# Weight-stationary tiles of a hybrid GLA and pooling backbone: all hi products of both units first, then all lo products

## Chip, core and metric

One Trainium2 chip, one core. The metric is the device time of one execution in microseconds. The kernel before takes 1768.76 us, the median of 3 runs (1768.55 to 1773.19).

## What is computed

One layer (DEPTH = 1) of a backbone on 256 latent tokens and 256 context tokens, width 2048, all in float32. Cut to what matters:

```python
sh_m, sc_m, gt_m, sh_f, sc_f, gt_f = split(silu(c) @ w_ada + b_ada, 6)   # the same for c_ctx
h_lat, h_ctx = x * (1 + sc_m) + sh_m, ctx * (1 + csc_m) + csh_m
q, k, v, g, a_lr, p, bg = split(h @ w_in)           # latent and context tokens
o_l = two-way chunked gated linear attention over latent tokens, started from the context's state
y_gla  = (rms_norm(o_l) * gain * silu(g)) @ w_gla_out
y_pool = (concat((box_mean(p_i) - p_i) @ w_pool_group[i]) * pool_scale) @ w_pool_out
mix = (sigmoid(bg_1) * y_gla + sigmoid(bg_2) * y_pool) @ w_out
x = layer_norm(2 ** 0.25 * x + gt_m * mix)
gate, up = split((x * (1 + sc_f) + sh_f) @ w_ffn_in)
x = layer_norm(2 ** 0.25 * x + gt_f * ((silu(gate) * up) @ w_ffn_out))
```

## The kernel before

**Precision by two parts.** A float32 factor is split into hi (rounded to TensorE's fp32r by ScalarE, L97) and lo, the rest (VectorE, L98). A product is hi*hi + hi*lo + lo*hi. Activations are kept as [hi | lo] side by side, 2 x 256 columns.

**Two kinds of matmul blocks.** In `nat_block` (L143 on; v, g, p, w_out, FFN out) activations are stationary and weights stream. In `ws_tile` (L116 to L134) weights are stationary: one tile gives 128 output columns, and its weights come in units of 128 x 1024, eight blocks of 128 rows of the contraction. For each unit the hi block streams the whole activation (a wide matmul, 512 columns, hi*hi and hi*lo, L127), the lo block only the activation's hi half (a narrow one, 256 columns, L131); `fold` (L136 to L141) adds the two halves of the PSUM bank afterwards, ScalarE first, then VectorE. `ws_tile` serves the stages k (8 tiles of two units, each for two activations, latent and context), q (8 tiles), gates, GLA output and pool output (16 column steps with two gate tiles, one GLA tile and one pool tile of a single unit each), and FFN in (44 steps with a gate tile and an up tile). All but the pool output's tiles have two units.

**Buffers.** `weights` (L101 on) issues the load of a unit into raw (L93, on SyncE's queue) and splits it into hi and lo. Each of raw, hi and lo has three buffers in the pool wp, shared by both kinds of blocks: a raw buffer comes free when lo is computed, a hi or lo buffer when TensorE has used it.

**What sets the order.** Instructions are written in program order and a scheduler orders each engine's queue by it and by what is ready; the splits are raised by 200 places (`tc.high_priority(PW)`), and some work is tied behind others (`tc.issue_after`). Beside the matmuls VectorE works off the rest of the adaLN projection in multiply-sums (L270, weights "ra" on SyncE's queue; in the FFN L930, "fa"), a few per tile. `bcast_cols` (L780 on) turns a modulation column into rows: VectorE writes diagonal tiles dg (L789), eight in all, and TensorE multiplies each with ones (L791); this happens at the start of w_out and again near the end of FFN in. Ahead of FFN in, `finish_mix` (L877 on) transposes the normed x, modulates it (L886, L889) and splits it into h, whose first half holds contraction blocks 0 to 7, whose second half 8 to 15.

Of the kernel before, what the change touches and what calls it, by code (L numbers as in the profile page):

```python
# [15 lines left out]
P = 128  # L16
D = 2048
KT = D // P
T = 256
# [39 lines left out]
def trunk(ctx, tc, small, masks, xT, ctxT, x_nat, lnrows, wdec, pmat, c_row,  # L59
# [5 lines left out]
    PE = nc.tensor  # L65
# [17 lines left out]
    def nm(s):  # L83
        cnt[0] += 1
        return f"{s}{cnt[0]}"

    def bank(kind="d"):
        pool, n = psum[-1]
        return pool.tile([P, 512], F32, tag=kind, bufs=n if kind == "d" else 8 - n, name=nm("ps"))

    def raw_unit(src, eng=None):
        r = wp.tile([P, U], F32, tag="raw", name=nm("raw"))
        (eng or nc.sync).dma_start(r, src)  # L93
        return r

    def split(full, hi, lo):
        S.activation(hi, full, AF.Copy)  # L97
        last_split[:] = [V.tensor_tensor(lo, full, hi.bitcast(F32), op=ALU.subtract)]  # L98
        return last_split[0]

    def weights(src):  # L101
        r = raw_unit(src)
        hi = wp.tile([P, U], F32R, tag="hi", name=nm("hi"))
        lo = wp.tile([P, U], F32R, tag="lo", name=nm("lo"))
        with tc.high_priority(PW):
            split(r, hi, lo)
        return hi, lo
# [8 lines left out]
    def ws_tile(srcs, acts, nk, kind="d"):  # L116

        outs = [bank(kind) for _ in acts]  # L120
        n = 0
        for src in srcs:
            hi, lo = weights(src)
            m = min(8, nk - n)
            for j in range(m):
                for o, act in zip(outs, acts):
                    PE.matmul(o, hi[:, j * P:(j + 1) * P], act(n + j), start=(n + j == 0), stop=(n + j == nk - 1),  # L127
                              skip_group_check=True)
            for j in range(m):
                for o, act in zip(outs, acts):  # L130
                    PE.matmul(o[:, :T], lo[:, j * P:(j + 1) * P], act(n + j)[:, :T], start=False, stop=(n + j == nk - 1),  # L131
                              skip_group_check=True)
            n += m
        return outs  # L134

    def fold(dst, o, scale=None):  # L136
# [6 lines left out]
    def nat_block(srcs, acts, k0=0, after=None, last=None, pre=None, cols=None):  # L143


        cols = cols or [(0, 512)] * len(acts)
        outs = [bank()[:, :c1 - c0] for c0, c1 in cols]
        n = k0
        end = k0 + 2 * len(srcs) - 1 if last is None else last
        for src in srcs:  # L150
            hi, lo = weights(src)
            if pre:
                pre()
            parts = [(j, o, act(n + j), j * 512 + c0, j * 512 + c1)
                     for j in range(2) for o, act, (c0, c1) in zip(outs, acts, cols)]
            for j, o, (ah, al), a, b in parts:
                PE.matmul(o, ah, hi[:, a:b], start=(n + j == k0), stop=False)  # L157
                PE.matmul(o, al, hi[:, a:b], start=False, stop=False)  # L158
            for j, o, (ah, al), a, b in parts:
                last_mm[:] = [PE.matmul(o, ah, lo[:, a:b], start=False, stop=(n + j == end))]  # L160
            n += 2
            if after:
                after()
        return outs
# [62 lines left out]
    with ExitStack() as c1:  # L227
# [27 lines left out]
        def ada(n, last=96):  # L255
            for _ in range(n):
                u = ada_next[0]
                if u >= last or not ada_pool:
                    return
                half, i = divmod(u, 48)  # L260
                if half not in silb:
                    silb[half] = p1.tile([P, U], F32, tag="silb", name=nm("silb"))
                    silu_row(silb[half], half, last_load[0])
                    return
                ada_next[0] += 1
                pool, tag, bufs = ada_pool[-1]
                r = pool.tile([P, U], F32, tag=tag, bufs=bufs, name=nm("ra"))
                nc.sync.dma_start(r, w_adaT[64 * half + i])
                with tc.issue_after(last_split[0].ins):
                    V.scalar_tensor_tensor(r, r, 1.0, silb[half], op0=ALU.mult, op1=ALU.mult,  # L270
                                           accum_out=mods[:, half, i:i + 1])
# [63 lines left out]
        def step(n=1):  # L335
            for _ in range(n):
                while pending:
                    try:
                        next(pending[0])
                        break  # L340
                    except StopIteration:
                        pending.pop(0)
# [24 lines left out]
        for n in GROUPS.values():  # L367
            for b in range(4):
                outs = nat_block([w_v[8 * b + a // 2 + i] for i in range(n // 2)], lat_s + ctx_s, k0=a,
                                 after=lambda: (step(STEPS[a]), ada(ADA[0].get(a, 0))))  # L370
# [46 lines left out]
        def kT_half(b):  # L417
            for lst, n in ((kT, "kT"), (kTc, "kTc")):
                if b == 0:
                    both[n] = sl(n)  # L420
                lst.append(both[n][:, b])
            for i in range(4):
                n = 2 * (4 * b + i)
                outs = ws_tile([w_k[n], w_k[n + 1]], [lat_m, ctx_m], KT)
                fold(kT[b][:, i, :], outs[0])
                fold(kTc[b][:, i, :], outs[1])
                if b == 0 and i == 0:
                    decay_rows()
                else:
                    ada(ADA[1])  # L430

        def qT_half(b):
            if b == 0:
                both["qT"] = sl("qT")
            qT.append(both["qT"][:, b])
            for i in range(4):
                n = 2 * (4 * b + i)
                o, = ws_tile([w_q[n], w_q[n + 1]], [lat_m], KT)
                fold(qT[b][:, i, :], o, HK ** -0.5)
# [262 lines left out]
        for b in range(2):  # L702
# [3 lines left out]
            for c in range(4):  # L706
                o = bank("g")
                for t in range(2):
                    PE.matmul(o[:, :T], p_blocks[b][:, t, c * P:(c + 1) * P], pm[:, t, c // 2, :],  # L709
                              start=(t == 0), stop=(t == 1))  # L710
# [26 lines left out]
        for ct in range(KT):  # L737
            o1, = ws_tile([w_bg[2 * ct + j] for j in range(2)], [lat_m], KT)
            yt = py.tile([P, 2 * T], F32, tag="tmp", bufs=2, name=nm("yt"))
            ys = py.tile([P, 2 * T], F32, tag="tms", bufs=2, name=nm("ys"))  # L740
            sg = yt[:, :T]
            fold(sg, o1)
            S.activation(sg, sg, AF.Sigmoid)
            if ct == 0:
                pool_out(0)
            o2, = ws_tile([w_bg[32 + 2 * ct + j] for j in range(2)], [lat_m], KT)
            sp = yt[:, T:]
            if ct == 0:
                pool_out(1)
            fold(sp, o2)  # L750
            last_sig[:] = [S.activation(sp, sp, AF.Sigmoid)]
            o3, = ws_tile([w_go[2 * ct + j] for j in range(2)], [moving(lambda kt: og[kt // 4][:, kt % 4])], KT)
            fold(ys[:, :T], o3)
            V.tensor_tensor(sg, ys[:, :T], sg, op=ALU.mult)
            o4, = ws_tile([w_po[ct]], [moving(lambda kt: yp[kt // 4][:, kt % 4])], 8)
            fold(ys[:, T:], o4)
            V.tensor_tensor(sp, ys[:, T:], sp, op=ALU.mult)
            V.tensor_tensor(sg, sg, sp, op=ALU.add)
            m = mT[ct // 8][:, ct % 8]
            split(sg, m[:, 0, :], m[:, 1, :])  # L760
            ada(ADA[2] if ct < 15 else 128)
# [86 lines left out]
    for b in range(3):  # L848
        outs = nat_block([w_o[8 * b + i] for i in range(8)], m_s)
# [91 lines left out]
    for b in range(3):  # L941
        outs = nat_block([w_fo[22 * b + i] for i in range(22)], hid_s)
# [6 lines left out]
    def finish_ffn(t):  # L949
        mean, rs = mv_rs[t]  # L950
        for b in range(4):
# [6 lines left out]
    outs = nat_block([w_fo[66 + i] for i in range(18)], [hid_s[t] for t, _, _ in PARTS], last=NF - 1,  # L958
                     cols=[c for _, *c in PARTS])
# [129 lines left out]
```

## Time and profile before

| | before |
|---|---|
| median of 3 runs | 1768.76 us (1768.55 to 1773.19) |
| the profiled execution's own time | 1772.31 us |
| its span, first to last instruction | 1770.5 us |
| mean granted TensorE clock | 0.992 |
| busy: TensorE, VectorE, ScalarE | 98%, 66%, 45% |
| moved from HBM | 389.58 MB, 221 GB/s over the span |

Stages in the profiled execution, from the span's start: adaLN and v to about 234 us, k to about 331, q with attention and g to about 590, gates and outputs to about 919, w_out and the first norm to about 1018, FFN in to about 1512, FFN out and the last norm to the end.

PE stands for TensorE's matmuls and PEld for its weight loads, DVE for VectorE, ACT for ScalarE, SP for SyncE. The end of a matmul in the records is modelled and overlaps the next one's start, so distances are taken from start to start. A bracket behind a row gives the idle time ahead of it and what ended it.

### The profile page before, as it was taken

What the parts mean: (1) busy time and instruction counts of PE and PEld (TensorE: products, weight loads), DVE (VectorE), ACT (ScalarE), POOL (GpSimd) and SP (SyncE); (2) the same over time, 40 slices, a digit from 0 to 9 for tenths busy, and PEclk for the clock granted to TensorE, in tenths of its full rate; (3) what the DMA queues carried; (4) which work ended last, traced back from release to release, by engine and by line L of the source; (5) the groups of instructions that cost most, each with busy time, mean ns of one, the idle gap of its engine ahead of it and who ended that gap; (6) DMA issues with size and microseconds to landing.
All of it is one profiled execution on the core that took longest, in us unless ns stands there. A gap on an engine that the chain in (4) does not pass through costs nothing.

```text
span 1770.5 us, 24390 instructions
## 1 busy us (share of the span) xinstructions
PE 1730.5 (98%) x9407; PEld 1451.1 (82%) x9407; DVE 1170.1 (66%) x1661; ACT 800.3 (45%) x1173; POOL 11.5 (1%) x28
## 2 busy tenths in 40 slices
PE   9999999999999999999999899999999999999996
PEld 5667888887777888888887788888888888888886
DVE  3667866667875677777776756666666666554455
ACT  2223132565874544444444554445444444443332
POOL 0000010000000000000000000000000000000000
PEclk9999999999999999999999999999999999999998
DMA  9797757443334478777785445577777766555553
GB/s 391 292 354 259 258 210 278 159 157 126 110 120 178 157 267 284 267 258 275 278 306 192 155 166 188 186 264 246 248 236 248 233 236 221 192 192 194 196 190 120
DMA packets 109059, 393.26 MB, mean 222 GB/s; under 512 B 12144, under 2 KB 12272, under 8 KB 108432
## 3 DMA queue, kind: packets, MB, share of 16 engines
q1 hardware_dynamic: 107424, 384.25, 62.4%
q0 software_dynamic: 1520, 7.47, 1.2%
q8 instruction: 73, 1.20, 0.3%
q14 instruction: 42, 0.34, 0.1%
HBM read 389.58 MB, written 2.10 MB: 221 GB/s over the span
## 4 chain that ended last, share of the span: by engine, by line
PE 87%; DVE 6%; ACT 3%; DMA 2%; issue 2%; SPq 0%; ACTq 0%; DVEq 0%
PE ps L127 34%; PE ps L131 18%; PE ps L157 10%; PE ps L160 10%; PE ps L158 10%; PE ps L293 2%; DVE lo L98 1%; DMA raw<-in_w_o 1%; ACT hi L97 1%; DMA raw<-in_w_fi 1%; PE ps L581 1%; DMA rw<-in_w_sh_sc 1%; PE ps L571 0%; PE ps L409 0%; PE ps L709 0%
## 5 line engine op out<-in xcount | busy, mean ns | idle before, releaser
L98 DVE TENSOR_TENSOR lo<-raw,hi 128x1024 fp32r<-128x1024 f32 x510 | 623.7, 1224 | 432.9 <-ACT hi L97 420.8
L97 ACT ACTIVATE hi<-raw 128x1024 fp32r<-128x1024 f32 x510 | 539.2, 1058 | 674.0 <-PE ps L127 275.1
L127 PE MATMUL ps<-h,hi 128*128 128x512 f32 x1408 | 353.4, 392 | 0.8 <-DVE h L98 0.8
L127 PEld LDWEIGHTS ps<-h,hi 128*128 128x128 f32 x1408 | 253.3, 189 | 46.5 <-DVE h L98 1.2
L127 PE MATMUL ps<-hl,hi 128*128 128x512 f32 x768 | 210.3, 392 | 0.0
L131 PEld LDWEIGHTS ps<-h,lo 128*128 128x128 f32 x1408 | 192.5, 190 | 13.9
L131 PE MATMUL ps<-h,lo 128*128 128x256 f32 x1408 | 196.8, 282 | 0.0
L127 PEld LDWEIGHTS ps<-hl,hi 128*128 128x128 f32 x768 | 139.4, 189 | 25.3
L157 PE MATMUL ps<-hi,hid 128*128 128x512 f32 (+1 forms) x372 | 134.9, 369 | 0.0
L158 PE MATMUL ps<-hi,hid 128*128 128x512 f32 (+1 forms) x372 | 134.0, 369 | 0.0
L157 PE MATMUL ps<-hi,hl 128*128 128x512 f32 x320 | 128.7, 403 | 2.7 <-ACT hi L97 2.7
L158 PE MATMUL ps<-hi,hl 128*128 128x512 f32 x320 | 126.6, 396 | 0.0
L270 DVE SCALAR_TENSOR_TENSOR ra<-ra,silb 128x1024 f32<-128x1024 f32 x96 | 114.4, 1221 | 13.0 <-DMA ra<-in_w_adaT 12.9
L131 PE MATMUL ps<-hl,lo 128*128 128x256 f32 x768 | 120.5, 282 | 0.0
L131 PEld LDWEIGHTS ps<-hl,lo 128*128 128x128 f32 x768 | 111.7, 190 | 6.9
L160 PE MATMUL ps<-lo,hl 128*128 128x512 f32 x320 | 93.0, 391 | 0.1
L160 PE MATMUL ps<-lo,hid 128*128 128x512 f32 x372 | 90.6, 369 | 0.0
L157 PEld LDWEIGHTS ps<-hi,hid 128*128 128x128 f32 x372 | 69.8, 188 | 12.1 <-DVE xt L812 0.2
L158 PEld LDWEIGHTS ps<-hi,hid 128*128 128x128 f32 x372 | 70.0, 188 | 11.9
L157 PEld LDWEIGHTS ps<-hi,hl 128*128 128x128 f32 x320 | 60.3, 189 | 22.5 <-issue 5.2
L348 DVE TENSOR_TENSOR v<-ps,v 128x512 f32<-128x512 f32 x80 | 50.7, 685 | 39.8 <-PE ps L160 39.7
L160 PEld LDWEIGHTS ps<-lo,hid 128*128 128x128 f32 x372 | 66.2, 188 | 11.9
(259 smaller groups left out, 2045.0 us busy)
## 6 DMA issues: line engine op xcount, KB each, us to landing
raw<-in_w_fi SPq DMA_DIRECT2D x176, 512.0 KB, 4.2
ra<-in_w_adaT SPq DMA_DIRECT2D x96, 512.0 KB, 4.9
raw<-in_w_fo SPq DMA_DIRECT2D x88, 512.0 KB, 4.3
rw<-in_w_sh_sc SPq DMA_DIRECT2D x64, 512.0 KB, 7.4
raw<-in_w_bg SPq DMA_DIRECT2D x64, 512.0 KB, 4.8
raw<-in_w_v SPq DMA_DIRECT2D x32, 512.0 KB, 5.7
raw<-in_w_g SPq DMA_DIRECT2D x32, 512.0 KB, 3.5
raw<-in_w_go SPq DMA_DIRECT2D x32, 512.0 KB, 4.2
```

The lines of the kernel that those rows point to most:

```text
L97: S.activation(hi, full, AF.Copy)
L98: last_split[:] = [V.tensor_tensor(lo, full, hi.bitcast(F32), op=ALU.subtract)]
L127: PE.matmul(o, hi[:, j * P:(j + 1) * P], act(n + j), start=(n + j == 0), stop=(n + j == nk - 1), skip_group_check=True)
L131: PE.matmul(o[:, :T], lo[:, j * P:(j + 1) * P], act(n + j)[:, :T], start=False, stop=(n + j == nk - 1), skip_group_check=True)
L157: PE.matmul(o, ah, hi[:, a:b], start=(n + j == k0), stop=False)
L158: PE.matmul(o, al, hi[:, a:b], start=False, stop=False)
L160: last_mm[:] = [PE.matmul(o, ah, lo[:, a:b], start=False, stop=(n + j == end))]
L270: V.scalar_tensor_tensor(r, r, 1.0, silb[half], op0=ALU.mult, op1=ALU.mult, accum_out=mods[:, half, i:i + 1])
L293: mm = PE.matmul(pr[32 * g:32 * g + 32, :256], sil[:, kt, :], r[:, 256 * g:256 * g + 256], start=(u == 0), stop=(u == KT // per - 1), skip ...
L348: V.tensor_tensor(dst, src, dst, op=ALU.add)
L581: PE.matmul(scc[:, t * T:(t + 1) * T], kst[:, c, t * P:(t + 1) * P], q4[:, c].rearrange("p t i -> p (t i)"), start=(d == 0 and c == 0 and ...
```

## The change

`ws_tile` fetches the weights of both units first (`ws`), then runs the products in two passes: s = 0 over all hi blocks of both units, s = 1 over all lo blocks. A one-unit tile keeps its order. Nothing else is edited, and the number and shapes of all instructions stay.

```diff
         outs = [bank(kind) for _ in acts]
-        n = 0
-        for src in srcs:
-            hi, lo = weights(src)
-            m = min(8, nk - n)
-            for j in range(m):
+        ws = [weights(src) for src in srcs]
+        for s in range(2):
+            for n in range(nk):
+                w = ws[n // 8][s][:, n % 8 * P:n % 8 * P + P]
                 for o, act in zip(outs, acts):
-                    PE.matmul(o, hi[:, j * P:(j + 1) * P], act(n + j), start=(n + j == 0), stop=(n + j == nk - 1),
-                              skip_group_check=True)
-            for j in range(m):
-                for o, act in zip(outs, acts):
-                    PE.matmul(o[:, :T], lo[:, j * P:(j + 1) * P], act(n + j)[:, :T], start=False, stop=(n + j == nk - 1),
-                              skip_group_check=True)
-            n += m
+                    if s == 0:
+                        PE.matmul(o, w, act(n), start=(n == 0), stop=(n == nk - 1), skip_group_check=True)
+                    else:
+                        PE.matmul(o[:, :T], w, act(n)[:, :T], start=False, stop=(n == nk - 1), skip_group_check=True)
         return outs
```

Lines behind it move up by four; a narrow matmul is L131 before and L129 after. TensorE's queue at the start of FFN in, before (h_8309 and h_8310 are the first and the second half of the activations; hi and lo with their number are one unit's two parts; a row ends with the number of equal matmuls):

```order
L127 MATMUL ps_8627<-h_8309,hi_8630 128x512 x4
L127 MATMUL ps_8676<-h_8309,hi_8679 128x512
L127 MATMUL ps_8627<-h_8309,hi_8630 128x512 x4
L131 MATMUL ps_8627<-h_8309,lo_8631 128x256 x8
L127 MATMUL ps_8676<-h_8309,hi_8679 128x512 x7
L131 MATMUL ps_8676<-h_8309,lo_8680 128x256 x7
L127 MATMUL ps_8627<-h_8310,hi_8652 128x512 x8
L131 MATMUL ps_8627<-h_8310,lo_8653 128x256 x8
L131 MATMUL ps_8676<-h_8309,lo_8680 128x256
L127 MATMUL ps_8676<-h_8310,hi_8701 128x512 x8
L131 MATMUL ps_8676<-h_8310,lo_8702 128x256 x8
```

The same place after:

```order
L127 MATMUL ps_8627<-h_8309,hi_8630 128x512 x4
L127 MATMUL ps_8676<-h_8309,hi_8679 128x512
L127 MATMUL ps_8627<-h_8309,hi_8630 128x512 x4
L127 MATMUL ps_8676<-h_8309,hi_8679 128x512 x7
L127 MATMUL ps_8627<-h_8310,hi_8636 128x512 x4
L127 MATMUL ps_8676<-h_8310,hi_8685 128x512 x3
L127 MATMUL ps_8627<-h_8310,hi_8636 128x512 x4
L129 MATMUL ps_8627<-h_8309,lo_8631 128x256 x8
L129 MATMUL ps_8627<-h_8310,lo_8637 128x256 x8
L127 MATMUL ps_8676<-h_8310,hi_8685 128x512 x5
L129 MATMUL ps_8676<-h_8309,lo_8680 128x256 x8
L129 MATMUL ps_8676<-h_8310,lo_8686 128x256 x8
```

The 15 narrow matmuls that stood ahead of the first use of h_8310 now stand behind it; in the later tiles 16 wide ones stand together, then 16 narrow ones. ScalarE's queue at that place (ht to h is a split of activations), before:

```order
L889 ACTIVATE ht_8619<-ps_8614,fcol 128x128 x4
L97 ACTIVATE hi_8701<-raw_8699 128x1024
L97 ACTIVATE h_8310<-ht_8607 128x4x128
L97 ACTIVATE h_8310<-ht_8619 128x4x128
L97 ACTIVATE hi_8729<-raw_8727 128x1024
L97 ACTIVATE hi_8751<-raw_8749 128x1024
```

And after:

```order
L885 ACTIVATE ht_8619<-ps_8614,fcol 128x128 x4
L97 ACTIVATE hi_8685<-raw_8683 128x1024
L97 ACTIVATE h_8310<-ht_8607 128x4x128
L97 ACTIVATE hi_8729<-raw_8727 128x1024
L97 ACTIVATE h_8310<-ht_8619 128x4x128
L97 ACTIVATE hi_8735<-raw_8733 128x1024
```

A weight split has moved between the two last splits of the activations. VectorE's queue at the second broadcast, near the end of FFN in (dg_12878 and dg_12881 are the first two diagonal tiles, ps_12821 the tile that TensorE ends just ahead of them), before:

```order
L789 TENSOR_TENSOR dg_12878<-sm,fs_12874 128x512
L98 TENSOR_TENSOR lo_12913<-raw_12910,hi_12912 128x1024
L140 TENSOR_TENSOR sg_12817<-ps_12772,sg_12817 128x256
L98 TENSOR_TENSOR lo_12935<-raw_12932,hi_12934 128x1024
L98 TENSOR_TENSOR lo_12962<-raw_12959,hi_12961 128x1024
L140 TENSOR_TENSOR sg_12817<-ps_12821,sg_12817 128x256
L789 TENSOR_TENSOR dg_12881<-sm,fs_12874 128x512
```

And after:

```order
L98 TENSOR_TENSOR lo_12913<-raw_12910,hi_12912 128x1024
L136 TENSOR_TENSOR sg_12817<-ps_12772,sg_12817 128x256
L785 TENSOR_TENSOR dg_12878<-sm,fs_12874 128x512
L98 TENSOR_TENSOR lo_12919<-raw_12916,hi_12918 128x1024
L98 TENSOR_TENSOR lo_12962<-raw_12959,hi_12961 128x1024
L136 TENSOR_TENSOR sg_12817<-ps_12821,sg_12817 128x256
L785 TENSOR_TENSOR dg_12881<-sm,fs_12874 128x512
```

The first dg has moved behind a lo tile and a fold, the second keeps its place on VectorE. On TensorE the second dg's matmul stood behind 8 wide and 4 narrow matmuls of the next tile; it now stands behind 11 wide ones:

```order
L787 MATMUL ps_12877<-dg_12878,onesq 128x512
L127 MATMUL ps_12909<-h_8309,hi_12912 128x512 x8
L127 MATMUL ps_12909<-h_8310,hi_12918 128x512 x3
L787 MATMUL ps_12877<-dg_12881,onesq 128x512
L127 MATMUL ps_12909<-h_8310,hi_12918 128x512 x4
```

The seventh dg's matmul there follows eight wide matmuls that need a new unit; on VectorE two lo tiles stand ahead of that dg.

## The prediction

> **What bounds the kernel now.** I read the page first (busy shares and the chain that ended last), then the busy time by stretches, then the timeline of short stretches and the chain in order of time. From the page:
>
> ```profile
> PE 1730.5 (98%) x9407; PEld 1451.1 (82%) x9407; DVE 1170.1 (66%) x1661; ACT 800.3 (45%) x1173; POOL 11.5 (1%) x28
> PE 87%; DVE 6%; ACT 3%; DMA 2%; issue 2%; SPq 0%; ACTq 0%; DVEq 0%
> ```
>
> TensorE is busy almost throughout and carries 87% of the chain. The busy time by stretches (columns: stretch and length, then busy time and count of PE, PEld, DVE, ACT and POOL, granted clock, DMA share, GB/s) shows the two long weight-stationary stages, the gate and output projections and the first FFN matrix:
>
> ```profile
> 590.00:919.00 329.00, 329.00 (x1887) 289.53 (x1886) 243.64 (x344) 162.32 (x239) 1.05 (x2) 1.00 0.78 265
> 1018.00:1512.00 494.00, 492.02 (x2811) 432.31 (x2812) 328.99 (x446) 244.28 (x366) 1.58 (x3) 1.00 0.66 224
> ```
>
> There PE hardly rests and the clock is full, so two things can move the time: how densely the matmuls follow each other, and a wait of PE that comes or goes. With one activation a unit is 8 wide matmuls (hi, 512 columns) and 8 narrow ones (lo, 256 columns), and a tile is two units. The timeline of the FFN stage (start, length modelled to the end of the last matmul, engine) shows four units, two tiles:
>
> ```profile
> 1099.81 2.00 PE L127 MATMUL ps<-h,hi 128*128 128x512 f32 x8
> 1101.65 1.12 PE L131 MATMUL ps<-h,lo 128*128 128x256 f32 x8
> ...
> 1105.39 2.00 PE L127 MATMUL ps<-h,hi 128*128 128x512 f32 x8
> ...
> 1110.98 2.00 PE L127 MATMUL ps<-h,hi 128*128 128x512 f32 x8
> ```
>
> From start to start a wide run takes 1.84 us and a unit 2.79; the two tiles take 11.17, so 5.59 each.
>
> **Term 1: fewer steps between narrow and wide.** The number and shapes of the matmuls stay. A two-unit tile now runs 16 wide and then 16 narrow, so one step of width in each direction goes. The kernel before already has that sequence in the k stage, where a unit feeds two activations. Single matmuls of one such unit in the timeline: the first wide one, the sixth, the first narrow one, and the first wide one of the next unit.
>
> ```profile
> 263.91 0.40 PE L127 MATMUL ps<-hl,hi 128*128 128x512 f32 x1
> ...
> 265.07 0.39 PE L127 MATMUL ps<-hc,hi 128*128 128x512 f32 x1
> ...
> 267.56 0.28 PE L131 MATMUL ps<-hl,lo 128*128 128x256 f32 x1
> ...
> 269.48 0.40 PE L127 MATMUL ps<-hl,hi 128*128 128x512 f32 x1
> ```
>
> The first five wide ones take 1.16 us, 0.232 each; the other eleven 2.49 us, 0.226 each. So a wide run starts slowly after a narrow one, by about 0.03 us in all, and pays that once, however long it is. For the size of the gain I take long stretches of the chain in order of time (start, length, run), each with the first and the last run:
>
> ```profile
> 264.07 3.65 PE ps L127 x16
> ...
> 325.31 3.65 PE ps L127 x16
> ...
> 605.83 1.84 PE ps L127 x8
> ...
> 809.74 1.84 PE ps L127 x8
> ```
>
> The upper pair spans 11 units of 16 + 16: 61.24 / 11 = 5.567 us. The lower pair spans 73 units of 8 + 8: 203.91 / 73 = 2.793, or 5.587 for two. The change should save 0.020 us a tile. Two-unit tiles: 8 in k, 8 in q, 32 + 16 in gates and GLA output, 88 in the FFN, 152 in all; the pool output's 16 tiles have one unit and stay as they are. The k tiles go from 16 + 16 twice to 32 + 32 and lose one step pair too. 152 x 0.020 = 3.0 us. Ends: 0, if the pair costs nothing where k's pattern isn't copied exactly, and 152 x 0.03 = 4.6, if the whole slow start is gained and the narrow runs give nothing back.
>
> The row sets the price. Against it stands the Trainium skill, "TensorE: Matmul & The Clock Gate", section "Back-to-back issue gap": a warm matmul follows the last after N/2.4 + 2.5 ns, by its columns alone. As an estimate from that page a tile of 16 wide and 16 narrow would take 5.20 us in either order, and term 1 would be zero; the trace has 5.59 and 5.57, so it agrees neither with the size nor with the order's being free.
>
> **Term 2: buffers that come free at other times.** raw, hi and lo have three buffers each. In the steady FFN stage ScalarE writes a hi tile as soon as PE has read the one three units back, and VectorE follows:
>
> ```profile
> 1107.48 1.06 ACT L97 ACTIVATE hi<-raw 128x1024 fp32r<-128x1024 f32 x1 [1.52 <-issue]
> 1108.58 1.23 DVE L98 TENSOR_TENSOR lo<-raw,hi 128x1024 fp32r<-128x1024 f32 x1 [1.36 <-ACT hi L97]
> 1113.78 0.40 PE L127 MATMUL ps<-h,hi 128*128 128x512 f32 x1
> raw<-in_w_fi SPq DMA_DIRECT2D x176, 512.0 KB, 4.2
> raw<-in_w_bg SPq DMA_DIRECT2D x64, 512.0 KB, 4.8
> ```
>
> The hi tile begun at 1107.48, after the run that started at 1105.39, is done at 1108.54 and needed three units later at 1113.78: 5.2 us early. Now the second unit's wide run comes 0.95 us earlier in its tile. Its hi buffer comes free at 1.84 after a tile's start and is needed at 5.57 + 1.84: 7.41 - 1.84 - 1.06, 4.5 us early. The first unit's lo buffer comes free only at 3.65 + 0.95 = 4.6 instead of 2.79. VectorE waits there with what is queued behind it (the other lo, the folds, the product, the adaLN multiply-sums), finishes at 5.8, and the raw buffer's next weights land 4.2 to 4.8 later, at 10.0 to 10.6. With ScalarE's 1.06 that unit is ready by 11.7 and needed three tiles on, at 16.7: 5 us to spare. So in steady state the new waits are hidden, at nothing; if the cover were gone, each tile would wait up to 0.95 us.
>
> **Term 3: entry of the FFN.** PE used to begin with both widths of two tiles on the first half of the new activations; the order now places only wide runs there, then the second half. In the trace:
>
> ```profile
> 1018.63 2.35 PE L127 MATMUL ps<-h,hi 128*128 128x512 f32 x9 [0.79 <-DVE h L98]
> 1021.77 1.78 PE L127 MATMUL ps<-h,hi 128*128 128x512 f32 x7
> 1024.22 2.05 PE L127 MATMUL ps<-h,hi 128*128 128x512 f32 x8
> 1021.17 1.07 ACT L97 ACTIVATE hi<-raw 128x1024 fp32r<-128x1024 f32 x1
> 1022.12 1.16 ACT L97 ACTIVATE h<-ht 128x512 fp32r<-128x512 f32 x2
> 1023.42 1.29 DVE L98 TENSOR_TENSOR h<-ht,h 128x512 fp32r<-128x512 f32 x2
> ```
>
> PE reached the second half at 1024.22, when the first of the two splits from 1023.42 was done (half of 1.29 later, 1024.07). Without the 15 narrow matmuls it gets there after nine (2.2 us) and seven (1.6): 1022.45. The VectorE split can now follow ScalarE's first half (1022.12 + 0.58 = 1022.7) without a lo tile ahead, and ends about 1023.4. PE waits 1.0 us. The next four columns stand behind a hi tile in ScalarE's queue; 1022.7 + 1.06 + 0.58 + 0.65 = 1025.0, while PE has 7 x 0.23 of other work, until 1025.05. I take +1.1. The ends are 0.6, if the split comes at once, and 2.0, if that next hi tile's buffer or weights are late.
>
> **Term 4: the second adaLN broadcast.** PE stood here for a diagonal tile (dg):
>
> ```profile
> 1488.08 0.40 PE L791 MATMUL ps<-dg,onesq 128*128 128x512 f32 x1
> 1488.32 2.00 PE L127 MATMUL ps<-h,hi 128*128 128x512 f32 x8
> 1492.13 0.50 PE L791 MATMUL ps<-dg,onesq 128*128 128x512 f32 x1 [1.35 <-DVE dg L789]
> 1488.39 1.22 DVE L98 TENSOR_TENSOR lo<-raw,hi 128x1024 fp32r<-128x1024 f32 x1
> 1489.91 1.23 DVE L98 TENSOR_TENSOR lo<-raw,hi 128x1024 fp32r<-128x1024 f32 x1 [0.30 <-ACT hi L97]
> 1491.06 0.42 DVE L140 TENSOR_TENSOR sg<-ps,sg 128x256 f32<-128x256 f32 x1
> 1491.39 0.68 DVE L789 TENSOR_TENSOR dg<-sm,fs 128x512 fp32r<-128x512 f32 x1
> ```
>
> VectorE had two lo tiles, a fold and the dg to do after the tile's end at 1488.08. Now the first of these lo tiles can start 0.95 before the tile's end, so the chain after it is one lo (1.23), a fold (0.33 to the next start) and the dg (0.68), ready 2.4 after the end. PE arrives after a broadcast matmul (0.24) and eleven wide ones (2.5), at 2.77. That wait goes. The seventh dg has two lo tiles ahead, the second released only when the narrow run ends: 1.23 + 0.68 = 1.9 against eight wide matmuls, 1.84; with hand-overs some 0.3 of new wait. Net -1.0; ends -1.35 (all gone) and +1.35 (the same wait at one more dg).
>
> **Sum.** -3.0 + 0 + 1.1 - 1.0 = -2.9 us. The profiled execution took 1772.31 (span 1770.5 and 1.8 around it), so a like execution would take 1769.4. It lies 3.6 above the median of the runs, 1768.76; its stretches show where such a difference can come from:
>
> ```profile
> 936.20:943.00 6.80, 6.13 (x14) 4.78 (x15) 5.44 (x9) 1.66 (x2) 0.00 (x0) 0.50 0.55 188
> ```
>
> After a long PE wait the clock is halved for 6.8 us with 6.1 us of PE work in it, some 3 us lost. The runs shown spread over 1768.55 to 1773.19. The weight-stationary stages aren't in that stretch, so the sum holds for the median: 1768.76 - 2.9 = 1765.9. A measurement of this kernel can tell about 0.3%, 5.3 us, from no change; the forecast is less than that.
>
> **Rivals.** (A) The order costs nothing: the step pair has no price outside the k stage, and terms 3 and 4 cancel: 1768.8. For it: the difference per tile is two hundredths of a microsecond. Against: 73 and 11 units agree with the single starts. Chance 0.18.
>
> (B) Slower: the later lo release becomes a late weight transfer in the gate and output stage, the one with DMA at 0.78. Its place is the raw chain of term 2. It decides when the 5 us to spare are used up, by adaLN multiply-sums ahead of lo on VectorE and their transfers ahead of raw on SP's queue. If then one tile of each of the 16 column steps waits 0.95, that is 15 us: 1765.9 + 15.2 = 1781. Against it: PE's 329.00 of 329.00 shows no wait there today. Chance 0.10.
>
> (C) Faster: both slow starts of a tile go, since a longer narrow run lets weight loads catch up: another 152 x 0.03 = 4.6 us, 1761.3. Against it: the k stage has narrow runs of 16 and still starts slowly. Chance 0.09.
>
> That the change does not do what it says is ruled out by the order. The forecast has 0.63.
>
> **Range and chances.** Lowest of the forecast: -4.6 + 0.6 - 1.35, 1763.4; highest: 0 + 2.0 + 1.35, 1772.1. Reaching towards (C) and to the half-clock scatter gives 1762.0 to 1773.0, with (B) left out. Faster by over 0.3% means under 1763.5: (C) and a little of the forecast's edge, 0.14. Slower, over 1774.1: (B) and a little, 0.12. Within: 0.74.
>
> **What would show it.** Right: two tiles in the FFN timeline 11.13 apart instead of 11.17; 16 wide then 16 narrow without waits; PE waiting about 1 us for h after the first 16 wide matmuls of the FFN; the 1.35 wait gone or small. Wrong: PE waits on hi or lo in the two stages, or SP's weight transfers landing just before ScalarE needs them; or a tile still at 5.59.

## The result: slower by 0.5 to 0.8%, most of it in FFN in

The kernel after took 1783.78 us, the median of 6 runs (1782.15 to 1790.9), beside 1771.91 for the kernel before in the same comparison: a ratio of 1.0076, 95% interval [1.0056, 1.0095]. The forecast was 1765.9 with a range to 1773.0, a gain of 2.9; measured is a loss of 11.9. A second comparison of the same two kernels, among the experiments below, gave 1.0053 [1.0039, 1.0067], so the loss is real, and its size is not known better than these two tell. The profiled execution took 1784.13 us (span 1782.3, clock 0.992), against 1772.31 (span 1770.5) before.

Where the 11.8 us of the two profiled executions lie, by the starts of the stages' first matmuls:

| stage | before, us | after, us | difference |
|---|---|---|---|
| up to the gates | 588.55 | 588.85 | +0.3 |
| gates and outputs | 318.79 | 319.45 | +0.7 |
| w_out, first norm | 111.29 | 113.34 | +2.0 |
| FFN in | 495.57 | 504.42 | +8.9 |
| FFN out, last norm | 256.25 | 256.22 | 0.0 |

From the page of the kernel after, the busy shares and the chain that ended last:

```profile
PE 1732.8 (97%) x9407; PEld 1452.9 (82%) x9407; DVE 1163.4 (65%) x1661; ACT 808.1 (45%) x1173; POOL 11.5 (1%) x28
PE 70%; DVE 12%; DMA 10%; ACT 5%; issue 3%; SPq 0%; DVEq 0%; ACTq 0%
```

TensorE is as busy as it was, but its part of the chain fell from 87% to 70%; VectorE, transfers and ScalarE took over 16 points. That is where a reader sees at once that a chain around TensorE, not TensorE itself, sets part of the time. The two stretches in which TensorE had hardly rested, between the same times as before (FFN in now begins 3.0 us later):

```profile
590.00:919.00 329.00, 324.06 (x1861) 285.64 (x1860) 237.31 (x339) 161.86 (x236) 1.05 (x2) 1.00 0.75 261
1018.00:1512.00 494.00, 487.38 (x2754) 426.16 (x2753) 320.84 (x442) 245.08 (x361) 1.58 (x3) 0.99 0.65 220
```

PE is now busy for 324.06 of 329.00 us and for 487.38 of 494.00. Most of the first gap is one wait of 3.8 us for hi at the start of w_out, at 915 us. PE's waits for hi on that line in the whole execution (total, times, longest; the longest is this one):

```profile
PE ps L153 <- ACT hi L97: 7.0, 4, 3.8
```

The wait for the first broadcast's dg, 25 us behind it, is 2.0 us shorter than before (4.2 to 2.2), and w_out as a whole lost 2.0.

**The matmuls are denser, as forecast.** The timeline of TensorE in the FFN, ahead of the adaLN sums:

```profile
1097.16 3.82 PE L127 MATMUL ps<-h,hi 128*128 128x512 f32 x16
...
1102.73 3.82 PE L127 MATMUL ps<-h,hi 128*128 128x512 f32 x16
...
1108.30 3.82 PE L127 MATMUL ps<-h,hi 128*128 128x512 f32 x16
```

Two tiles are 11.14 apart instead of 11.17, 5.57 each.

**The tiles wait, once the adaLN sums run.** The sums run in FFN steps 12 to 39; the first late tile starts at 1286 us, in step 23, and all late ones lie between it and step 39. Two tile starts in the same timeline, 81 tiles apart:

```profile
1035.93 1.32 PE L127 MATMUL ps<-h,hi 128*128 128x512 f32 x5
...
1493.68 2.68 PE L127 MATMUL ps<-h,hi 128*128 128x512 f32 x11
```

457.75 us for 81 tiles of 5.567 (450.9) leaves 6.8 us of waits. In the kernel before, the same count of tiles takes 81 x 5.587 us and no more: no waits at all. How the wait arises stands in the chain in order of time (start, length, what), here one turn of it in the kernel after:

```profile
1311.14 1.23 DVE fa L926 x2
1312.37 1.15 DVE lo L98
...
1313.57 5.93 DMA raw<-in_w_fi
...
1319.61 1.07 ACT hi L97
...
1320.70 1.23 DVE lo L98
1321.92 0.35 DVE sg L136
...
1322.29 0.43 DVE sg L905
...
1322.75 0.43 ACT hid L97
...
1323.54 1.23 DVE fa L926 x2
```

No row of it is TensorE's. It is a closed loop through VectorE's queue and the raw buffers, one turn to an FFN step: the adaLN sum (fa), the lo product queued behind it, the load that this product lets go (a raw buffer comes free), that load's hi and lo, and behind that lo on VectorE the up tile's fold, the product, the hid split and the next adaLN sum. One turn takes 1323.54 - 1311.14 = 12.40 us; TensorE needs 2 x 5.567 = 11.13 for the step. Without the transfer the loop is 12.40 - 5.93 = 6.47 long, so it is hidden as long as the transfer takes less than 4.66 us, and costs what the transfer takes above that, first out of the lead that the buffers give, then out of TensorE's time.

The other turns bear this out. In the 21 turns of this trace with one sum and its load, the transfer takes 4.2 to 5.9 us and the rest of the turn 6.5 to 6.8; 13 of the 21 turns are longer than 11.13, the longest 12.54. In the last two, when no adaLN load is left to issue, the transfer takes 3.4 and 3.5 and the turn 9.8 and 9.9. The kernel before at the same place has TensorE alone in its chain:

```profile
1311.31 0.95 PE ps L131 x8
1312.27 1.84 PE ps L127 x8
```

Its VectorE had the lo product ahead of the hid split and of the sum, so neither stood in such a loop (the timeline of before):

```profile
1311.29 0.42 DVE L909 TENSOR_TENSOR sg<-sg 128x256 f32<-128x256 f32 x1
1312.49 1.23 DVE L98 TENSOR_TENSOR lo<-raw,hi 128x1024 fp32r<-128x1024 f32 x1 [0.78 <-ACT hi L97]
1313.63 0.42 DVE L98 TENSOR_TENSOR hid<-sg,hid 128x256 fp32r<-128x256 f32 x1
1313.97 1.22 DVE L930 SCALAR_TENSOR_TENSOR fa<-fa,silf 128x1024 f32<-128x1024 f32 x1
```

And its loads were spread more evenly. SyncE's issues, before:

```profile
1310.95 3.12 SPq L93 DMA_DIRECT2D raw<-in_w_fi  x2
1315.22 0.33 SPq L928 DMA_DIRECT2D fa<-in_w_adaT  x1
1316.54 0.33 SPq L93 DMA_DIRECT2D raw<-in_w_fi  x1
```

And after:

```profile
1312.39 0.33 SPq L924 DMA_DIRECT2D fa<-in_w_adaT  x1
1313.57 2.90 SPq L93 DMA_DIRECT2D raw<-in_w_fi  x3
```

Four loads of 512 KB within 4 us now, then none for five. ScalarE's waits for weights in the whole execution say the same, before (total us, times, longest):

```profile
ACT hi L97 <- DMA raw<-in_w_fi: 24.5, 15, 3.6
```

and after:

```profile
ACT hi L97 <- DMA raw<-in_w_fi: 137.9, 88, 5.6
```

**The entry of FFN in, and the second adaLN broadcast.** The entry after, by the timeline and by the stretch:

```profile
1021.64 5.88 PE L127 MATMUL ps<-h,hi 128*128 128x512 f32 x16 [0.78 <-DVE h L98]
1025.88 1.06 ACT L97 ACTIVATE hi<-raw 128x1024 fp32r<-128x1024 f32 x1 [1.58 <-PE ps L127]
1026.85 0.61 ACT L97 ACTIVATE h<-ht 128x512 fp32r<-128x512 f32 x1
1028.24 0.50 PE L127 MATMUL ps<-h,hi 128*128 128x512 f32 x1 [0.73 <-DVE h L98]
1021.50:1025.50 4.00, 3.86 (x9) 3.09 (x10) 2.05 (x6) 1.87 (x5) 0.00 (x0) 0.50 0.00 0
```

PE waits about 0.9 us for h at 1028.24, as forecast; but the first nine matmuls run at a granted clock of 0.50, 427 ns each instead of 227, which costs 2 us more and was in no term. At the broadcast:

```profile
1501.62 1.23 DVE L98 TENSOR_TENSOR lo<-raw,hi 128x1024 fp32r<-128x1024 f32 x1 [0.61 <-ACT hi L97]
1503.10 0.68 DVE L785 TENSOR_TENSOR dg<-sm,fs 128x512 fp32r<-128x512 f32 x1
1503.84 0.50 PE L787 MATMUL ps<-dg,onesq 128*128 128x512 f32 x1 [1.69 <-DVE dg L785]
```

The wait for dg is 1.69, not gone: the lo product ahead of it waited for a hi tile that was late. The raw loads issued at 1484.2 and 1485.3 had taken 7.4 and 7.9 us, beside two loads of norm rows of 1 MB each on GpSimd's queue.

So FFN in adds up: -1.8 (88 tiles by 0.020) + 6.8 (steps) + 1.0 (wait for h) + 2.0 (half clock) + 0.8 (broadcast) = +8.8, measured +8.85.

### The profile page after: what moved, and what is told of

Same layout as the page of the kernel before. It is cut to its first block, busy times and chain, and to the rows that moved or that the text cites. A ratio compares the mean times of both kernels' runs of the same rounds, so it can differ in the third digit from the quotient of the medians.

```text
span 1782.3 us, 24433 instructions
## 1 busy us (share of the span) xinstructions
PE 1732.8 (97%) x9407; PEld 1452.9 (82%) x9407; DVE 1163.4 (65%) x1661; ACT 808.1 (45%) x1173; POOL 11.5 (1%) x28
## 4 chain that ended last, share of the span: by engine, by line
PE 70%; DVE 12%; DMA 10%; ACT 5%; issue 3%; SPq 0%; DVEq 0%; ACTq 0%
PE ps L127 23%; PE ps L129 12%; PE ps L153 10%; PE ps L156 9%; PE ps L154 9%; DVE lo L98 5%; DMA raw<-in_w_fi 4%; DMA raw<-in_w_bg 2%; ACT hi L97 2%; DMA raw<-in_w_o 2%; PE ps L289 2%; DMA raw<-in_w_po 1%; DVE ra L266 1%; DVE fa L926 1%; PE ps L577 1%
## 5 line engine op out<-in xcount | busy, mean ns | idle before, releaser
L98 DVE TENSOR_TENSOR lo<-raw,hi 128x1024 fp32r<-128x1024 f32 x510 | 616.7, 1222 | 419.6 <-ACT hi L97 332.1
L127 PE MATMUL ps<-h,hi 128*128 128x512 f32 x1408 | 339.9, 393 | 2.2 <-DVE h L98 1.5
L127 PEld LDWEIGHTS ps<-h,hi 128*128 128x128 f32 x1408 | 259.8, 189 | 55.1 <-DVE h L98 2.6
L127 PE MATMUL ps<-hl,hi 128*128 128x512 f32 x768 | 202.9, 391 | 0.6 <-ACT hi L97 0.6
L129 PEld LDWEIGHTS ps<-h,lo 128*128 128x128 f32 x1408 | 181.4, 191 | 11.1 <-DVE lo L98 3.9
L129 PE MATMUL ps<-h,lo 128*128 128x256 f32 x1408 | 185.1, 283 | 2.5 <-DVE lo L98 2.5
L129 PE MATMUL ps<-hl,lo 128*128 128x256 f32 x768 | 114.0, 283 | 0.0
L129 PEld LDWEIGHTS ps<-hl,lo 128*128 128x128 f32 x768 | 106.6, 191 | 3.4
L154 PEld LDWEIGHTS ps<-hi,hid 128*128 128x128 f32 x372 | 70.0, 188 | 11.8
L156 PEld LDWEIGHTS ps<-lo,hid 128*128 128x128 f32 x372 | 66.2, 188 | 11.9
```

The costliest lines, as they stand in the source:

```text
L127: PE.matmul(o, w, act(n), start=(n == 0), stop=(n == nk - 1), skip_group_check=True)
L129: PE.matmul(o[:, :T], w, act(n)[:, :T], start=False, stop=(n == nk - 1), skip_group_check=True)
```

## Experiments

Theory A: the order on VectorE makes the loss (the paired, late release of the lo buffers moves a lo product behind the hid split and the adaLN sum). Theory B: the late release by TensorE alone starves the buffers. Theory C: loads that bunch on a queue or on the DMA engines. "Step waits" below is the excess over 81 tiles, found as above; "FFN in" runs from its first matmul to FFN out's first. Ratios are of the timed runs against the kernel before, with 95% intervals.

| run | ratio | FFN in, us | step waits, us |
|---|---|---|---|
| before | 1 | 495.57 | 0.0 |
| after | 1.0076 [1.0056, 1.0095] | 504.42 | 6.8 |
| e1 before, VectorE's order of after | 1.0048 [1.0031, 1.0064] | 505.37 | 7.8 |
| e2 after, no loads and sums | 1.0012 [0.9999, 1.0025] | 493.85 | 0.0 |
| e3 after, no loads | 1.0022 [1.0012, 1.0031] | 497.34 | 0.0 |
| e4 after, no sums | 1.0025 [1.0016, 1.0035] | 497.78 | 0.0 |
| e5 second unit lo, hi | 0.9997 [0.9986, 1.0009] | 495.99 | only at step 41 |
| e6 after, fetch late | 1.0041 [1.0027, 1.0054] | 505.07 | 6.4 |
| e7 before, fetch early | 0.9999 [0.9990, 1.0008] | 494.28 | 0.0 |
| e8 after, sums later | 1.0027 [1.0016, 1.0038] | 499.30 | 0.0 |
| e9 after again | 1.0053 [1.0039, 1.0067] | 502.07 | 3.7 |
| e10 after, loads on another queue | 1.0020 [1.0007, 1.0034] | 502.43 | 2.8 |
| e11 after, first FFN tile as before | 1.0040 [1.0025, 1.0054] | 504.99 | 7.3 |
| e12 e5, steps 40 to 43 as before | 0.9996 [0.9987, 1.0006] | 495.04 | none seen |
| e13 two passes but in the FFN | 0.9995 [0.9986, 1.0003] | 495.55 | 0.0 |
| e14 two passes in the FFN alone | 1.0020 [1.0011, 1.0029] | 499.97 | 4.0 |
| e15 e8, steps 40 to 43 as before | 1.0013 [1.0004, 1.0022] | 493.75 | none seen |

**e1: VectorE's order alone, in the kernel before.** TensorE's order, and so the release at 2.79 us, stays.

```diff
+        tie[:] = [sums, None] if 12 < f <= 40 else []      # sums: the step's adaLN sum
         ou, = ws_tile([w_fi[2 * (NF + f) + j] for j in range(2)], [h2_m], KT, "g")
 # in weights(), for the second unit of the up tile
+            with tc.issue_after(t.ins):
                 V.tensor_tensor(lo, r, hi.bitcast(F32), op=ALU.subtract)
```

> Kernel before, with TensorE's order untouched; in FFN steps 13 to 40 VectorE alone is given the order of the kernel after: the lo product of the up tile's second unit is tied behind the step's hid split and adaLN sum. The stage FFN in took 495.6 us before and 504.4 us after. Theory A (VectorE's order: a lo product behind the hid split and the sum starves the raw ring): the stage takes 502 to 506 us, the whole 1776 to 1782. Theory B (the lo buffers' late, paired release by TensorE itself) and theory C (the loads bunch on the DMA engines because the releases are paired): the release is at 2.79 us into the tile here, the lo product waits 1 us at most, the stage takes 495 to 497 us, the whole 1769 to 1773.

FFN in took 505.4 us, and the whole 1779.2: theory A's numbers. PE's busy time in a stretch of the FFN (columns as above), before and in this run:

```profile
1130.00:1480.00 350.00, 350.00 (x2008) 308.06 (x2008) 237.64 (x324) 170.14 (x253) 1.58 (x3) 1.00 0.71 242
```

```profile
1130.00:1480.00 350.00, 345.28 (x1964) 300.82 (x1963) 229.37 (x316) 168.55 (x247) 1.58 (x3) 1.00 0.69 232
```

Its chain shows the same loop, and how the transfer decides its length:

```profile
1304.87 1.23 DVE fa L936 x2
...
1307.30 4.70 DMA raw<-in_w_fi
...
1316.04 1.23 DVE fa L936 x2
...
1318.47 6.40 DMA raw<-in_w_fi
```

With 4.70 the turn takes 1316.04 - 1304.87 = 11.17, of which 6.47 are the rest of the loop, the same number as in the kernel after; here TensorE's step is 11.17, so that turn cost nothing and the one with 6.40 does.

**e2, e3, e4: take the loads and sums away, together and one by one.** In order, in the kernel after (e2 drops the whole group, whose columns of mods are then 0; e3 leaves out 29 of the 32 loads, not the 30 of its expectation, and its sums read what the buffers hold; e4 leaves the sums out):

```diff
-                nc.sync.dma_start(r, w_adaT[64 * half + 48 + i])            # e3, but for the first three
-                    V.scalar_tensor_tensor(r, r, 1.0, silf[half], ...)      # e4
+                    V.tensor_copy(mods[:, half, 48 + i:49 + i], r[:, 0:1])  # e4
```

> Kernel after without the 32 loads and 32 multiply-sums of the last adaLN gate in FFN steps 12 to 39 (left out: the columns 48 to 63 of mods, which are set to 0). If the loss needs these loads or sums (theories A and C, and B with them as its trigger): the stage FFN in takes 493 to 495 us instead of 504.4, TensorE's waits on hi and lo there are gone, the whole 1771 to 1774. If the two-pass order alone starves TensorE: the stage stays at 502 us or more.

> Kernel after with all 32 multiply-sums of the last adaLN gate on VectorE, but 30 of their 32 loads left out (the sums read what the buffers hold, so the columns 50 to 63 of that gate's mods are not the weights' sums). Theory A (VectorE's order and its time): the stage FFN in stays at 501 to 505 us. Theory C (the load of 512 KB bunched with the raw loads, on SP's queue and the DMA engines): it falls to 493 to 496 us, and raw loads land in 4.2 to 4.9 us again instead of 5.9.

> Kernel after with all 32 loads of the last adaLN gate, but each multiply-sum on VectorE (1.22 us) replaced by a copy of one column at the same place (left out: the sums of mods' columns 48 to 63). Theory A (VectorE's time ahead of the lo products): the stage FFN in falls to 493 to 497 us. Theory C (the bunched loads): it stays at 500 to 505 us.

e2 came out as expected. Its FFN in even shows the prediction's terms: -1.8 for the tiles, no step waits, +1.2 at the entry and -1.2 at the broadcast, 1.7 us less than before. e3 and e4 each gave half an answer to both theories: either one ends all step waits, and both stay 3.5 to 3.9 us above e2 by the half clock at the entry (in both, not in e2) and the broadcast. The stretch of e3, and of e4:

```profile
1130.00:1480.00 350.00, 350.00 (x2015) 309.39 (x2014) 234.12 (x324) 177.77 (x253) 1.57 (x3) 1.00 0.59 198
```

```profile
1130.00:1480.00 350.00, 350.00 (x2012) 309.26 (x2011) 204.20 (x293) 175.74 (x255) 1.58 (x3) 1.00 0.73 241
```

Neither theory A nor theory C alone says that; the loop does. Without the sum (1.23, a copy of 0.15 in its place) its fixed part falls, by subtraction, to 5.4 and a transfer of up to 5.7 is hidden. Without the loads the loop's transfer takes 3.3 to 3.8 us (once 4.35), and 6.47 + 3.8 = 10.3 is hidden under 11.13. The loss needs both the sum in the loop and the slow transfer that its load brings. It is a sum over one threshold, not two costs that add.

**e6 and e7: the place of the fetch.** The diff also moved the second unit's load and split ahead of the tile in the program. e6 puts that back in the kernel after, e7 makes it alone in the kernel before.

```diff
-        ws = [weights(src) for src in srcs]        # e6
+        ws = []
...
+                if s == 0 and n % 8 == 0:
+                    ws.append(weights(srcs[n // 8]))
```

> Kernel after with one thing put back: the second unit's load and split stand in the program where the kernel before has them, behind the first unit's hi products, and not ahead of the tile's first matmul. If the place of the fetch in the program is a cause: the stage FFN in falls from 504.4 us towards 495, ratio 1.000 to 1.003. If TensorE's order is the cause (through the release of the lo buffers, theories A, B and C): nothing changes, FFN in 502 to 506 us, ratio 1.006 to 1.009.

> Kernel before with the other half of the change alone: both units of a tile are fetched ahead of its matmuls, TensorE's order stays hi, lo, hi, lo. If the place of the fetch is a cause: ratio 1.004 or more, FFN in 500 us or more. If only TensorE's order is: ratio 0.999 to 1.001, FFN in 495 to 496 us.

e7 is no change. In e6 FFN in stays at 505.1 us with 6.4 us of step waits. The ratio, 1.0041, is under what was expected, but e9 puts the unchanged kernel after at 1.0053, and the intervals overlap. The place of the fetch does nothing; the order on TensorE does.

**e5 and e12: as few step pairs, but an early release.**

```diff
+            for s in ((0, 1) if u % 2 == 0 else (1, 0)):     # unit u; e12 keeps (0, 1) in steps 40 to 43
```

> Another order with as few changes between wide and narrow matmuls as the kernel after has: the first unit of a tile runs hi then lo, the second lo then hi, so the two lo passes lie side by side and so do the hi passes of neighbouring tiles, but the first unit's lo buffer is free after 2.8 us as in the kernel before, and VectorE's order is that of before. If the loss comes only from VectorE's order and the bunched loads that the late release brings (theories A and C): TensorE keeps its 0.020 us a tile, the stage FFN in takes 493 to 495 us (before 495.6), the whole 1765 to 1768, ratio 0.997 to 0.999. If long runs of wide or of narrow matmuls cost by themselves, or the gain of a step pair is not real: ratio 1.000 to 1.003.

> The order of the run with the second unit lo then hi, in all two-unit tiles but those of FFN steps 40 to 43, which keep before's order (that run lost 1.5 us there, where hi for the second unit came late behind the adaLN broadcast). Theory A and C: no bunch, 0.020 us a tile kept: ratio 0.998 to 0.9995, the whole 1767 to 1770. If hi's later release costs elsewhere as well: ratio 0.9995 to 1.001.

Both have before's place of the fetch, which e7 showed to be no cause. The expectation was two thirds right. VectorE's order and the loads are before's, a tile takes 5.567, and the FFN's loss is gone; but the whole didn't get faster: 0.9997 and 0.9996. In e5, 1.5 us went in one wait for lo at step 41, where the hi buffer of the second unit, now free only at the tile's end, was filled late (ScalarE waited 6.0 us for it); in e12, which avoids that, eight matmuls at the FFN's entry ran at half clock in the profiled execution. The 3 us of step pairs, 0.17%, are of the size of the interval: that they reach the end is neither shown nor excluded.

**e8 and e15: leave TensorE's two passes, move the sums.** Each sum goes behind the next step's gate fold, so that it stands behind the pair of lo products and outside the loop.

```diff
-                with tc.issue_after(lo_ins.ins):
+            with tc.issue_after(gate.ins):        # gate: the next step's gate fold
                     V.scalar_tensor_tensor(r, r, 1.0, silf[half], ...)
```

> Kernel after with TensorE's order untouched; in the FFN steps 12 to 39 each multiply-sum of the last adaLN gate is moved on VectorE from behind the step's hid split to behind the next step's gate fold, so that the two lo products that now stand behind it go first. Its load follows it. Theory A (VectorE's order ahead of the pair of lo products makes the bunch): FFN in 494 to 497 us instead of 504.4, the loss ahead of the FFN stays (about 3 us), the whole 1773 to 1775. If the paired release of the lo buffers bunches the loads wherever the sum stands (theories B and C): FFN in 500 us or more.

> Two-pass order with the sums of FFN steps 12 to 39 behind the next gate fold, as in the run with the late sums, and before's order in the tiles of FFN steps 40 to 43, where that run lost 3.8 us in waits of the adaLN broadcast. If the two-pass order is worth its step pairs once nothing stands ahead of its lo products: FFN in 493 to 497 us (the entry's 3 us may stay), ratio 0.998 to 1.001. If a loss stays that no sum explains: ratio 1.002 or more.

The step waits vanish, with all loads and sums done:

```profile
1130.00:1480.00 350.00, 350.00 (x2014) 309.39 (x2013) 238.52 (x324) 175.44 (x255) 1.57 (x3) 1.00 0.73 241
```

So the late, paired release alone (theory B) starves nothing. FFN in was above theory A's 494 to 497 because of 2 us of half clock at the entry and waits for dg at the broadcast (2.2 and 1.1 us). e15 takes those waits away: FFN in 493.75, the shortest of all, in an execution that was the shortest of its eleven; the median of the eleven is still 0.13% above before.

**e9, e10, e11.** The kernel after again; its 32 adaLN loads on GpSimd's queue; and its first FFN tile in before's order.

```diff
-                nc.sync.dma_start(r, w_adaT[64 * half + 48 + i])      # e10
+                nc.gpsimd.dma_start(r, w_adaT[64 * half + 48 + i])
...
+   order=[(s, range(8 * u, 8 * u + 8)) for u in range(2) for s in range(2)] if f == 0 else None   # e11
```

> The kernel after, unchanged, a second time beside the others: every theory expects what it took the first time, ratio 1.006 to 1.009, stage FFN in 503 to 506 us. If its time moves by more than that between chips, the loss is not one fixed sum but depends on when the bunches begin.

> Kernel after with the 32 loads of the last adaLN gate issued on GpSimd's queue, not on SP's between the raw loads; VectorE's order, TensorE's order and the bytes stay. If the raw loads are late because they stand behind such a load on SP's queue while it waits for its buffer (25 waits, 61 us): FFN in falls to 494 to 498 us, the whole 1772 to 1776. If they are late because a bunch of four loads of 512 KB shares the DMA engines, whatever the queue: FFN in stays at 501 to 506 us.

> Kernel after with one tile put back, the first gate tile of the FFN, which runs hi, lo, hi, lo again. At the entry the kernel after loses 0.9 us in a wait for h behind the first eight wide matmuls, and 2 us more in nine wide matmuls at 427 ns (half clock) where before has 227. If both come from the second unit's hi pass asking for h 1.1 us earlier: the entry falls back by 3 us, to before's. If the half clock is the chip's and only meets this place: the wait goes (0.9 us) and the nine matmuls at 427 ns stay, or go, whatever the order. The FFN's later loss stays: FFN in 500 to 504 us.

e9: the same kernel lost 3.7 us in the steps of its profiled execution instead of 6.8, its first late tile starting at 1374 us instead of 1286. Some turns are over the threshold and some under it, by the transfer, and they must first use up the lead that the steps before the sums had built: in the first trace of the kernel after, a tile's first hi unit is done 5.6 to 6.0 us ahead of its use just before the sums, and 0.05 us ahead at 1320. So when the loop begins to cost depends on small things. e10 is inconclusive: its time fell to 1.0020, with an interval that lies below e9's, so the queue seems to matter; but its profiled execution, the longest of the ten, has the bunch, the loop and 2.8 us of step waits. In it the loop's transfer still takes 4.1 to 5.5 us with the adaLN load on another queue, so there the place on SyncE's queue is not what makes it slow. e11 missed: the half clock stays (seven matmuls), and the wait for h stays as well, 0.6 us, later. In ScalarE's queue the second half of h stands behind a hi tile that waits 1.3 us for its buffer in e11 (1.58 in the row at 1025.88 above), and in e11 that tile's lo (1.23) stands ahead of it on VectorE as well.

**e13 and e14: two passes in one part alone.**

```diff
-    def ws_tile(srcs, acts, nk, kind="d"):
+    def ws_tile(srcs, acts, nk, kind="d", two=True):      # e13: FFN calls with two=False; e14: the reverse
```

> Two-pass order in every two-unit tile but those of the FFN; the FFN has before's order on TensorE and on VectorE. If the loss is the FFN's (theory A, with the sums and loads there): FFN in 494.3 to 496 us, what is left is the step pairs' gain in the gates stage (64 tiles by 0.020 us) against some 2.5 us lost around w_o in the kernels with the two-pass order so far, ratio 0.999 to 1.002. If the stages' losses are equal in kind and size: ratio 1.003 or more.

> Two-pass order in the FFN's tiles alone, all else in before's order. If the FFN makes nearly all of the loss: FFN in 502 to 506 us, the stages ahead of it as before, ratio 1.003 to 1.006. If the gates stage must have shifted the buffers first: FFN in below 499 us, ratio below 1.002.

Outside the FFN alone the change costs nothing (0.9995); in the FFN alone it makes the loop (4.0 us of step waits) and 1.0020, below what was expected. 0.9995 and 1.0020 don't add up to 1.0053 or 1.0076. What of the whole comes only from both together, some 0.4 to 0.6%, is explained in part at most. Two costs recur in the profiles of the ten kernels with two passes in all parts (after, e2, e3, e4, e6, e8 to e11 and, but for its last steps, e15). One is TensorE's wait for hi at the start of w_out: 3.5 to 4.3 us in all ten, 0.6 in e13, none in before and e14; it leaves w_out at 111.9 to 115.3 us, beside 109.8 to 112.2 in before, e1, e7, e13 and e14. The other is the half clock at the FFN's entry, 2 us, in eight of the ten and in none of those five. Why both come only with two passes in both parts no run shows, and ahead of the FFN the profiled executions of kernels with the same instructions up to there (after, e2, e3, e4, e8, e9, e10) reach its first matmul anywhere from 1018.6 to 1024.4 us, so one profile of each can't settle how much of the time that is.

## Why the prediction was wrong

**Term 1, -3.0 for the step pairs: right in its price.** In the FFN a tile that doesn't wait takes 5.567 us in every kernel with runs of 16, and 5.587 in every kernel with runs of 8, 0.020 apart. The estimate from the Trainium skill's formula ("TensorE: Matmul & The Clock Gate", "Back-to-back issue gap"), which that section gives for an isolated matmul, is 5.20 in either order and agrees with neither. What failed was to think that what TensorE saves reaches the end.

**Term 2, "the new waits are hidden, at nothing": the step that failed.** Three things in its working fell. It read the lo product as keeping its place, with the folds, the product and the sums queued behind it; VectorE's queue has the hid split and the sum ahead of it instead, and this was to be read in the order. It took the landing of a load from a trace with more evenly spaced loads (4.2 to 4.8, medians); the loop's load, 1.2 us behind an adaLN load, takes 4.2 to 5.9. And it held 5 us of lead against a single wait of 0.95. The lead is a stock: what counts is whether one turn of the loop fits into TensorE's step, and the slack of that is 11.13 - 6.47 - 4.2, under half a microsecond. Above it, a turn takes up to 1.4 us from the stock, and then from TensorE: 6.8 us of waits in FFN steps 23 to 39, where the prediction had nothing.

**Rival B had the mechanism**, its condition word for word ("adaLN multiply-sums ahead of lo on VectorE and their transfers ahead of raw on SP's queue"), but in the wrong stage: it was placed in the gates, where the DMA share is highest, and not in the FFN, where sum, hid split and lo products share one step. Its price, 15 us, was too high for the 6.8 measured, and its chance of 0.10 was argued down by PE's full busy time in the kernel before, which says nothing about what is left once VectorE's order changes.

**Term 3, +1.1 at the entry: right** for the wait (0.9 us at one place and 0.1 behind it). The half clock, 2 us, was outside its ends of 0.6 and 2.0.

**Term 4, -1.0 at the broadcast: wrong sign.** It came out at +0.8, because the lo product ahead of dg waited for a late hi tile, behind raw loads of 7.4 and 7.9 us beside those of the norm rows. The loop had ended by then, and a tile's first hi unit was 5.8 us early again one tile sooner, so this is not term 2's miss again. In e2 the norm rows came some 310 us earlier, the second dg without a wait, and the stretch was 1.2 us shorter, as forecast. But in e7, with before's order on TensorE, it was 1.3 shorter too: the wait that this term hoped to save is not fixed to that order.

**No term** stood for the start of w_out, where hi was 3.8 us late and the stage lost 2.0. Why hi is late there stays open.

## What to carry to other kernels

When an edit changes which buffer comes free first, read each engine's new queue for what now stands ahead of the producer, and close the loop: add up one turn through queue, load and split, and hold it against the consumer's step, not against the lead. A lead of several microseconds hides one late tile, but not a loop that is one microsecond too long. And when removing either of two suspects removes the whole loss, think of a threshold before thinking of two causes.

## What the hardware showed that was not expected

With an adaLN load of 512 KB issued 1.2 us ahead and two raw loads close behind, the loop's raw load of 512 KB took 4.2 to 5.9 us in the kernel after; in e3, without the adaLN load, 3.3 to 3.8, once 4.35. With the same spacing of issues it took 5.93 at 1313.57 and 4.22 at 1338.08, and what makes that difference no run shows.

Runs of matmuls at a granted clock of 0.50 appear behind waits of TensorE, and not always at the same ones. At the FFN's entry they come in nine of the thirteen profiled executions of kernels with the two-pass order or e5's in the FFN, seven to eleven wide matmuls at 427 ns each, and in none of the four with before's order there (before, e1, e7, e13), though the first matmul starts 1.2 to 1.4 us behind the last transpose in all seventeen. The Trainium skill ("TensorE: Matmul & The Clock Gate", "What's actually happening") has the array's clock set by how busy TensorE was in a window that runs free of the kernel, so that the place of a transition depends on where in the window the work falls. By its "Wait — 56ns, not 53.3ns?" 512 columns at half clock take 426.7 ns. The 427 ns here agree, and the scatter fits; no run here shows the window itself. Whether the two-pass order makes the entry more likely to be caught, or only shifted it into such a phase, no run here decides.
